# Elementwise work of a four-mixer transformer layer moved from GpSimd to VectorE and ScalarE

## The chip, the cores and the metric

The kernel runs on one core of one Trainium2 chip. The metric is device microseconds of one execution. A core has five engines, each with its own queue of instructions in a fixed order: PE (TensorE, the matmuls; PEld is its weight load), DVE (VectorE), ACT (ScalarE), POOL (GpSimd) and SP (SyncE, which here only issues DMA transfers). An instruction that needs another engine's result waits at the head of its queue, and everything behind it on that engine waits too.

## The reference

One layer over 256 tokens of width 2048, all in f32. Four mixers read slices of `h @ w_in`; their outputs go through a gated merge, an output projection and a feed-forward network with a short convolution.

```python
h = rms_norm(x, attn_norm)
(gla.., lru.., nsa.., rwkv_feat, merge_gate) = split_cols(h @ w_in, IN_SPLITS)
y_a, y_b, y_c, y_d = gla_mixer(..), rglru_mixer(..), nsa_mixer(..), rwkv7_mixer(..)
gates = sigmoid(merge_gate).reshape(B, S, 4, D_MODEL)
merged = zeros_like(x)
for n, y in enumerate((y_a, y_b, y_c, y_d)):
    merged = merged + gates[:, :, n] * (y @ w_branch[n])
x = x + merged @ w_out
u = causal_dwconv(rms_norm(x, ffn_norm) @ ffn_up, ffn_conv_w, ffn_conv_b)
x = x + (silu(u_gate) * u_val) @ ffn_down

# rwkv7_mixer, per head and token, state 64 x 64
k  = k * (1 + (a - 1) * k_a);  kk = normalized(k * k_k)
sa = einsum('ij,j->i', state, -kk_t)
state = state * w_t + outer(sa, kk_t * a_t) + outer(v_t, k_t)
y_t = einsum('ij,j->i', state, r_t)

# gla_mixer, per chunk of 64 tokens
scores = einsum('td,sd,tsd->ts', q, k, exp(b_t - b_s))   # causal
```

## The kernel before

**The stream.** Almost all of the time is weight matmuls. `stream` (L300) loads f32 weights with SP as tiles `raw` of 128x1024 (5 buffers). Each half of a raw is split in two for precision: ACT casts it to `wh` (L327), DVE subtracts to get the rest `wl` (L328), 128x512 each, 6 buffers of either. `group_A` (L337) feeds PE with them: for each 128 rows of the contraction and each 128 output columns a matmul with wh (128x512 moving) and one with wl (128x256), all into a PSUM tile `acc`. One wl, 128x512, holds two blocks of two column pieces, so it serves eight matmuls in a row, four with wh and four with wl. If a wl comes late, PE stands.

**What rides on it.** The mixers' own work lies between these matmuls. In the RWKV7 mixer, `rwkv_kk` (L657) makes kk, k2 and rk, tiles of 128x4x256. `rwkv_blocks` (L714) builds sixteen 64x64 matrices N per half of the partitions, sends them through memory (`n_rows`) to lay 128 blocks of 32x32 on the partitions, and inverts each by a recursion of 31 steps, two operations a step (L742, L743):

```python
self.tt(t, nb[...k + 1:, k], zb[:, k, 0:w], MULT, nc.gpsimd)
self.tt(zb[:, k + 1:, 0:w], zb[:, k + 1:, 0:w], t, ADD, nc.gpsimd)
```

Each reads what the one before wrote. The result goes through memory again (`z_rows`, L746, to Zb), is transposed on DVE in `rwkv_corners` (L758), and feeds 64 small matmuls P on PE. The chain of the state over four chunks (`rwkv_chain`, L818, with the decay sd) follows. In `gla` (L1037) eight levels each compute ge on DVE, its absolute value and exponential on ACT, two products qe (one half on DVE, the other on POOL), 32 small matmuls gs on PE and two masked copies on DVE (L1090). In `nsa` (L1276) the attention's weights pt are scaled by the gates (L1324). `branch` (L1352) adds every branch into merged.

**What sets the order.** The kernel is written in a program order with five bands of priority (load, split, evac, mix, big). A scheduler runs a timeline of its own over it, with its own durations of each instruction, and fixes the order on every engine. Only the transpose of Z (and one other) keeps its place in the program order (L758), between the groups of the first merge. A changed engine or duration therefore moves other instructions too.

Of the kernel before, what the change touches and what calls it, by code (L numbers as in the profile page):

```python
# [14 lines left out]
AF = mybir.ActivationFunctionType  # L15
# [5 lines left out]
P = 128  # L21
# [204 lines left out]
class Kern:  # L226
# [430 lines left out]
    def rwkv_kk(self):  # L657
        nc = self.nc
        hs = self.cst("hs")
        self.hs = hs  # L660
        kk = self.m4("kk")
        for j in range(4):
            nc.gpsimd.tensor_scalar(kk[:, j, :], self.rw_k[:, j, :], self.col("k_k", j), None, op0=MULT)
        sq = self.m4("kksq")
        self.act(sq, kk, AF.Square)

        def pre(out, ps):
            self.ts(out, ps, 1e-24, None, ALU.max)
            self.act(out, out, AF.Sqrt)

        def post(jp, pb):
            self.tt(kk[:, 2 * jp:2 * jp + 2, :], kk[:, 2 * jp:2 * jp + 2, :], pb, MULT)

        self.head_norm(sq, hs, pre, post)
        self.rw_kk = kk

        hka = self.sm([P, 4], "hka")
        self.ts(hka, self.col("k_a", 0, 4), 0.5, None, MULT)
        oka = self.sm([P, 4], "oka")
        self.ts(oka, hka, -1.0, 1.0, MULT, ADD)  # L680
        k2 = self.m4("k2")
        for j in range(4):
            self.act(k2[:, j, :], self.rw_tha[:, j, :], AF.Identity, scale=hka[:, j:j + 1], bias=oka[:, j:j + 1])
        self.tt(k2, k2, self.rw_k, MULT, nc.gpsimd)
        self.rw_k2 = k2
        bb = self.m4("bb")
        self.ts(bb, self.rw_tha, 0.5, 0.5, MULT, ADD)
        self.tt(bb, bb, kk, MULT)
        self.rw_b = bb
        rk = self.m4("rk")  # L690
        self.tt(rk, self.rw_r, k2, MULT, nc.gpsimd)
        self.rw_rk = rk

    def rwkv_ops(self, c):
# [19 lines left out]
    def rwkv_blocks(self, Ts):  # L714


        nc = self.nc
        H = (slice(0, 64), slice(64, 128))
        n = self.m4("N", 16)
        nd = self.pools["d"].tile([16, P, 64], F32, name="n_rows")  # L720
        zd = self.pools["d"].tile([2, 2, 16, 2, 32, 16], F32, name="z_rows")
        for c in range(4):
            ar, bk = Ts[c]["ar"], Ts[c]["bk"]
            pv = self.ps("N")[:, 0:256].rearrange("p (j s) -> p j s", j=4)
            for j in range(4):
                for h in H:
                    self.mm(pv[h, j, :], ar[h, j, 0, :], bk[h, j, 0, :])
            sl = slice(4 * c, 4 * c + 4)
            self.tt(n[:, sl, :], pv, self.cst("mN").unsqueeze(1).broadcast_to([P, 4, 64]), MULT)
            nc.sync.dma_start(nd[sl].rearrange("u p s -> p u s"), n[:, sl, :])  # L730
        nb = self.sb("mg", [P, 32, 32], F32, "N32")
        zb = self.m2("Z32", 32)
        tmp = self.m1("ztmp", 1)[:, 0, :]
        nc.sync.dma_start(self.flat(zb), self.A["z0"])
        for hf in range(2):
            for q in range(2):
                o = 64 * hf + 32 * q
                nc.sync.dma_start(nb[o:o + 32], nd.rearrange("u (a t) s -> (u a) t s", a=2)[:, 32 * q:32 * q + 32, 32 * q:32 * q + 32])
        for k in range(31):
            r, w = 31 - k, min(k + 1, 16)  # L740
            t = tmp[:, 0:r * w].rearrange("p (r w) -> p r w", r=r)
            self.tt(t, nb[:, k + 1:, k:k + 1].broadcast_to([P, r, w]), zb[:, k:k + 1, 0:w].broadcast_to([P, r, w]), MULT, nc.gpsimd)  # L742
            self.tt(zb[:, k + 1:, 0:w], zb[:, k + 1:, 0:w], t, ADD, nc.gpsimd)  # L743
        y = self.m4("Zb", 16)
        nc.gpsimd.memset(y, 0.0)
        nc.sync.dma_start(zd.rearrange("f q u a t s -> (f q u a) t s"), zb)  # L746
        for a in range(2):
            for q in range(2):
                for hf in range(2):
                    o, c0 = 64 * a + 32 * q, 32 * q + 16 * hf  # L750
                    nc.sync.dma_start(y[o:o + 32, :, c0:c0 + 16], zd[hf, q, :, a].rearrange("u t s -> t u s"))
        self.rw_n, self.rw_zb = n, y
# [65 lines left out]
    def rwkv_chain(self, c, T, st):  # L818
# [20 lines left out]
        if c < 3:  # L839
# [8 lines left out]
            else:  # L848
                sd = self.m1("sd")
                ec = self.rw_ec[:, :, c:c + 1]  # L850
                self.tt(sd, st, ec.broadcast_to([P, 4, 64]), MULT, nc.gpsimd)
                self.tt(new, sd, ps, ADD)
        ps = g4("Yo")
        for j in range(4):
# [182 lines left out]
    def gla(self):  # L1037
# [28 lines left out]
        for lv in range(8):  # L1066
# [6 lines left out]
            self.act(e, e, AF.Exp, scale=-1.0 / 16)  # L1073
            qe = self.m4("qe")
            self.tt(qe[:, 0:2, :], qk[:, 0:2, :], e, MULT)
            self.tt(qe[:, 2:4, :], qk[:, 2:4, :], e, MULT, nc.gpsimd)
            if lv == 6:
                for par in range(2):
                    h = H[par]
# [196 lines left out]
    def nsa(self):  # L1276
# [24 lines left out]
        for tt in range(2):  # L1301
# [19 lines left out]
            self.tt(lt, lt, ws[:, :, 0:1].broadcast_to([P, 4, 15]), MULT)  # L1321
            for h in range(4):
                for a in range(2):
                    nc.gpsimd.tensor_scalar(pts[h][:, a, :], pts[h][:, a, :], ws[:, h, 1 + a:2 + a], None, op0=MULT)  # L1324
            srcs = [(None, 0)] + [(a, s) for a in range(2) for s in range(tt + 1)]
            po = self.ps("no")
            for n, (a, st) in enumerate(srcs):
# [24 lines left out]
    def branch(self, n, cg, h, yk, th, first):  # L1352
        ps = self.group_A(self.stream(self.A["w_branch"], (4 * n + cg) * 2 + h, 256, 4), 4, yk)
        with self.at("evac"):
# [6 lines left out]
            else:  # L1361
                b = self.sb("fd", [P, 2, 256], F32, "b")
                self.fold(b, ps)
                self.stt(t, t, 1.0, b, ADD, MULT)
                self.tt(m, m, t, ADD, self.nc.gpsimd)

    def tick(self, most=0):

# [185 lines left out]
```

## Time and profile before

| | |
|---|---|
| median of three runs | 1607.89 us |
| the three runs | 1608.23, 1607.89, 1599.86 us |
| the profiled execution, its own time | 1600.85 us |
| its span in the trace | 1599.1 us |
| PE, DVE, ACT, POOL busy | 98%, 78%, 60%, 11% of the span |
| mean granted TensorE clock | .988 of full speed |

The profiled execution is one of its own, and its span is 1.75 us under its time. In the rows below an operation is read as line, engine, operation, output and inputs by the program's names, shape, and a count. A table by line gives after the bar the busy time in us and the mean of one operation in ns, then the idle time before them and what ended it. A busy time is that in which at least one such operation is under way, so it can be less than count times mean when neighbours overlap. A table of stretches gives the window and its length, then for each engine the busy us and, in brackets, the number of instructions. PEclk is the TensorE clock granted, 1.00 for 2.4 GHz and 0.5 for 1.2 GHz. In a timeline the brackets at the end name the idle time ahead of the instruction and what ended it.

### The profile page before, as it was taken

To read this page: it belongs to the slowest core of one execution; us is meant where nothing else is said; L and a number is where in the kernel's file an instruction comes from. 1 tells how busy PE (TensorE), PEld (TensorE's weight loads), DVE (VectorE), ACT (ScalarE), POOL (GpSimd) and SP (SyncE) were. 2 spreads that over 40 slices of the span, in tenths; PEclk is the share of its full clock that TensorE was granted. 3 is DMA by queue.
4 is the path that set the end of the run, shared out by engine and by line. 5 is a ranking of instruction groups with operands and counts; after the bars stand their busy time and mean duration, and the time that the engine had idled before them with its cause. 6 is when DMAs were issued, how large, how long until landed. Compare 5 with 4: busy or idle time off the path is not lost.

```text
span 1599.1 us, 27514 instructions
## 1 busy us (share of the span) xinstructions
PE 1566.2 (98%) x10062; PEld 1414.7 (88%) x10062; DVE 1248.2 (78%) x2034; ACT 955.8 (60%) x1685; POOL 168.5 (11%) x178
## 2 busy tenths in 40 slices
PE   8999889999899999999999999999999999999998
PEld 7998778888789889899999999999999999999998
DVE  8798965485887768777797888886678886688875
ACT  6777543365665566656566666664466664566653
POOL 3113900000211201311121100000000000000000
PEclk9999988999999999999999999999999999999999
DMA  7656353256356766456676666666666666666663
GB/s 270 233 160 210 121 168 97 96 173 205 124 166 204 239 220 201 156 180 202 202 251 201 194 209 199 201 200 206 198 200 202 201 201 200 202 204 198 200 224 131
DMA packets 95801, 305.80 MB, mean 191 GB/s; under 512 B 20021, under 2 KB 20789, under 8 KB 95664
## 3 DMA queue, kind: packets, MB, share of 16 engines
q1 hardware_dynamic: 94448, 299.60, 58.3%
q0 software_dynamic: 1216, 4.43, 0.8%
q8 instruction: 79, 1.29, 0.3%
q14 instruction: 58, 0.48, 0.1%
HBM read 300.32 MB, written 3.67 MB: 190 GB/s over the span
## 4 chain that ended last, share of the span: by engine, by line
PE 89%; DVE 3%; POOL 3%; issue 2%; DMA 1%; ACT 1%; SPq 1%; DVEq 0%; POOLq 0%; ACTq 0%
PE acc L297 83%; POOL Z L289 2%; POOL ztmp L289 1%; DVE wl L328 1%; PE G L297 1%; PE Yo L297 1%; PE M L297 1%; DMA raw<-in_cmp 0%; PE no L297 0%; DMA raw<-in_wf_r 0%; ACT wh L327 0%; DVE qe L289 0%; PE r L297 0%; PE c L297 0%; PE sc L297 0%
## 5 line engine op out<-in xcount | busy, mean ns | idle before, releaser
L328 DVE TENSOR_TENSOR wl<-raw,wh 128x512 fp32r<-128x512 f32 x1096 | 788.1, 728 | 281.6 <-ACT wh L327 275.8
L297 PE MATMUL acc<-h,wh 128*128 128x512 f32 x3008 | 1000.3, 385 | 1.3 <-DVE th L289 0.9
L327 ACT CAST wh<-raw 128x512 fp32r<-128x512 f32 x1096 | 671.6, 619 | 507.3 <-PE acc L297 474.8
L297 PE MATMUL acc<-h,wl 128*128 128x256 f32 x3008 | 826.9, 275 | 6.1 <-DVE wl L328 6.1
L297 PEld LDWEIGHTS acc<-h,wh 128*128 128x128 f32 x3008 | 571.1, 190 | 83.5 <-issue 1.7
L297 PEld LDWEIGHTS acc<-h,wl 128*128 128x128 f32 x3008 | 579.9, 193 | 10.6 <-DVE wl L328 7.0
L297 PE MATMUL acc<-f,wh 128*128 128x512 f32 x704 | 230.7, 382 | 0.0
L297 PE MATMUL acc<-f,wl 128*128 128x256 f32 x704 | 191.9, 273 | 0.0
L297 PEld LDWEIGHTS acc<-f,wh 128*128 128x128 f32 x704 | 133.1, 189 | 18.5
L297 PEld LDWEIGHTS acc<-f,wl 128*128 128x128 f32 x704 | 135.2, 192 | 0.0
L297 PE MATMUL acc<-mg,wh 128*128 128x512 f32 x256 | 83.9, 382 | 0.3 <-DVE b L289 0.3
L286 DVE SCALAR_TENSOR_TENSOR u<-u,prm,u 128x254 f32<-128x254 f32 (+1 forms) x176 | 80.8, 480 | 0.5
L297 PE MATMUL acc<-mg,wl 128*128 128x256 f32 x256 | 69.6, 273 | 0.0
L289 POOL TENSOR_TENSOR merged<-merged,th 128x512 f32<-128x512 f32 x24 | 41.7, 1736 | 243.7 <-DVE th L286 243.7
L297 PEld LDWEIGHTS acc<-mg,wh 128*128 128x128 f32 x256 | 48.3, 189 | 7.3 <-DVE b L289 0.6
L289 DVE TENSOR_TENSOR xres<-xres,acc 128x512 f32<-128x512 f32 (+1 forms) x66 | 44.0, 668 | 9.9 <-PE acc L297 7.8
L283 ACT ACTIVATE u<-u,prm 128x256 f32<-128x256 f32 x88 | 48.1, 594 | 2.6 <-DVE u L289 0.8
L297 PEld LDWEIGHTS acc<-mg,wl 128*128 128x128 f32 x256 | 49.1, 192 | 0.1
L297 PE MATMUL acc<-wh,h 128*128 128x512 f32 (+1 forms) x128 | 30.2, 328 | 0.0
L289 DVE TENSOR_TENSOR u<-u,rs 128x512 f32<-128x512 f32 x44 | 30.1, 684 | 0.0
L289 DVE TENSOR_TENSOR u<-u,acc 128x512 f32<-128x512 f32 x44 | 30.0, 681 | 0.0
L283 ACT ACTIVATE th<-th 128x512 f32<-128x512 f32 (+1 forms) x33 | 21.3, 645 | 13.5 <-DVE th L289 12.4
(400 smaller groups left out, 1329.3 us busy)
## 6 DMA issues: line engine op xcount, KB each, us to landing
raw<-in_w_up SPq DMA_DIRECT2D x176, 512.0 KB, 4.3
raw<-in_w_gate SPq DMA_DIRECT2D x128, 512.0 KB, 3.6
raw<-in_w_down SPq DMA_DIRECT2D x88, 512.0 KB, 4.2
raw<-in_w_branch SPq DMA_DIRECT2D x32, 512.0 KB, 3.9
raw<-in_w_out SPq DMA_DIRECT2D x32, 512.0 KB, 4.2
raw<-in_wf_k SPq DMA_DIRECT2D x8, 512.0 KB, 4.4
raw<-in_wf_misc SPq DMA_DIRECT2D x8, 512.0 KB, 4.4
raw<-in_wf_lx SPq DMA_DIRECT2D x8, 512.0 KB, 4.3
```

The source lines that it names most:

```text
L283: return self.nc.scalar.activation(out, in_, func, bias=bias, scale=scale, **kw)
L286: return self.nc.vector.scalar_tensor_tensor(out, in0, scalar, in1, op0=op0, op1=op1)
L289: return (eng or self.nc.vector).tensor_tensor(out, a, b, op=op)
L297: return self.nc.tensor.matmul(out, lhsT, rhs, start=start, stop=stop, **kw)
L327: nc.scalar.copy(wh, rb)
L328: nc.vector.tensor_tensor(wl, rb, wh.bitcast(F32), op=SUB)
```

## The change

Seven pieces of elementwise work change their engine. From POOL to DVE go the product of k2 with k and rk (two of 128x1024), the recursion's 62 operations, the state decay sd (two small ones), the second half of every qe (eight of 128x512) and the addition into merged (24 of 128x512). From POOL to ACT go the four scalings of kk (128x256) and the sixteen scalings of pt (128x128 and 128x256). What is computed stays the same.

```diff
--- before.py
+++ after.py
@@ -660,7 +660,7 @@
         self.hs = hs
         kk = self.m4("kk")
         for j in range(4):
-            nc.gpsimd.tensor_scalar(kk[:, j, :], self.rw_k[:, j, :], self.col("k_k", j), None, op0=MULT)
+            self.act(kk[:, j, :], self.rw_k[:, j, :], AF.Copy, scale=self.col("k_k", j))
         sq = self.m4("kksq")
         self.act(sq, kk, AF.Square)
 
@@ -681,14 +681,14 @@
         k2 = self.m4("k2")
         for j in range(4):
             self.act(k2[:, j, :], self.rw_tha[:, j, :], AF.Identity, scale=hka[:, j:j + 1], bias=oka[:, j:j + 1])
-        self.tt(k2, k2, self.rw_k, MULT, nc.gpsimd)
+        self.tt(k2, k2, self.rw_k, MULT)
         self.rw_k2 = k2
         bb = self.m4("bb")
         self.ts(bb, self.rw_tha, 0.5, 0.5, MULT, ADD)
         self.tt(bb, bb, kk, MULT)
         self.rw_b = bb
         rk = self.m4("rk")
-        self.tt(rk, self.rw_r, k2, MULT, nc.gpsimd)
+        self.tt(rk, self.rw_r, k2, MULT)
         self.rw_rk = rk
 
     def rwkv_ops(self, c):
@@ -739,8 +739,8 @@
         for k in range(31):
             r, w = 31 - k, min(k + 1, 16)
             t = tmp[:, 0:r * w].rearrange("p (r w) -> p r w", r=r)
-            self.tt(t, nb[:, k + 1:, k:k + 1].broadcast_to([P, r, w]), zb[:, k:k + 1, 0:w].broadcast_to([P, r, w]), MULT, nc.gpsimd)
-            self.tt(zb[:, k + 1:, 0:w], zb[:, k + 1:, 0:w], t, ADD, nc.gpsimd)
+            self.tt(t, nb[:, k + 1:, k:k + 1].broadcast_to([P, r, w]), zb[:, k:k + 1, 0:w].broadcast_to([P, r, w]), MULT)
+            self.tt(zb[:, k + 1:, 0:w], zb[:, k + 1:, 0:w], t, ADD)
         y = self.m4("Zb", 16)
         nc.gpsimd.memset(y, 0.0)
         nc.sync.dma_start(zd.rearrange("f q u a t s -> (f q u a) t s"), zb)
@@ -848,7 +848,7 @@
             else:
                 sd = self.m1("sd")
                 ec = self.rw_ec[:, :, c:c + 1]
-                self.tt(sd, st, ec.broadcast_to([P, 4, 64]), MULT, nc.gpsimd)
+                self.tt(sd, st, ec.broadcast_to([P, 4, 64]), MULT)
                 self.tt(new, sd, ps, ADD)
         ps = g4("Yo")
         for j in range(4):
@@ -1073,7 +1073,7 @@
             self.act(e, e, AF.Exp, scale=-1.0 / 16)
             qe = self.m4("qe")
             self.tt(qe[:, 0:2, :], qk[:, 0:2, :], e, MULT)
-            self.tt(qe[:, 2:4, :], qk[:, 2:4, :], e, MULT, nc.gpsimd)
+            self.tt(qe[:, 2:4, :], qk[:, 2:4, :], e, MULT)
             if lv == 6:
                 for par in range(2):
                     h = H[par]
@@ -1321,7 +1321,7 @@
             self.tt(lt, lt, ws[:, :, 0:1].broadcast_to([P, 4, 15]), MULT)
             for h in range(4):
                 for a in range(2):
-                    nc.gpsimd.tensor_scalar(pts[h][:, a, :], pts[h][:, a, :], ws[:, h, 1 + a:2 + a], None, op0=MULT)
+                    self.act(pts[h][:, a, :], pts[h][:, a, :], AF.Copy, scale=ws[:, h, 1 + a:2 + a])
             srcs = [(None, 0)] + [(a, s) for a in range(2) for s in range(tt + 1)]
             po = self.ps("no")
             for n, (a, st) in enumerate(srcs):
@@ -1362,7 +1362,7 @@
                 b = self.sb("fd", [P, 2, 256], F32, "b")
                 self.fold(b, ps)
                 self.stt(t, t, 1.0, b, ADD, MULT)
-                self.tt(m, m, t, ADD, self.nc.gpsimd)
+                self.tt(m, m, t, ADD)
 
     def tick(self, most=0):
```

POOL's queue goes from 165 rows to 65, DVE's from 1912 to 2001, ACT's from 1582 to 1588. The scheduler also moves what lies around. On DVE, where the recursion begins (N_166 is N laid out anew, Z_167 the result being built up, rw_v the values of the mixer), the difference of after against before:

```order
 L328 TENSOR_TENSOR wl_1937<-raw_1922,wh_1936 128x512
-L286 SCALAR_TENSOR_TENSOR rw_v_1951<-F_1734,prm,rw_v_1951 128x255
+L286 SCALAR_TENSOR_TENSOR rw_v_1951<-F_1734,prm,rw_v_1951 128x255 x2
+L289 TENSOR_TENSOR ztmp_1115<-N_166_1113,Z_167_1114 128x31
+L289 TENSOR_TENSOR Z_167_1114<-Z_167_1114,ztmp_1115 128x31
+L289 TENSOR_TENSOR ztmp_1115<-N_166_1113,Z_167_1114 128x60
+L289 TENSOR_TENSOR Z_167_1114<-Z_167_1114,ztmp_1115 128x30x2
+L289 TENSOR_TENSOR ztmp_1115<-N_166_1113,Z_167_1114 128x87
+L289 TENSOR_TENSOR Z_167_1114<-Z_167_1114,ztmp_1115 128x29x3
 L328 TENSOR_TENSOR wl_1965<-raw_1962,wh_1964 128x512
+L289 TENSOR_TENSOR ztmp_1115<-N_166_1113,Z_167_1114 128x112
+L289 TENSOR_TENSOR Z_167_1114<-Z_167_1114,ztmp_1115 128x28x4
```

The first step, which waits for N's way through memory, now stands in DVE's queue ahead of wl_1965 and of everything behind it. From there on one to three steps stand between two wl, the last just behind wl_2689.

On DVE at the transpose of Z (merged_321 and th_1960 belong to the first merge), before:

```order
L328 TENSOR_TENSOR wl_2461<-raw_2446,wh_2460 128x512
L289 TENSOR_TENSOR merged_321_2316<-merged_321_2316,acc_2289 128x512
L286 SCALAR_TENSOR_TENSOR merged_321_2316<-th_1960,merged_321_2316 128x512
L758 STREAM_TRANSPOSE Z_2320<-Zb_1183 128x1024
L328 TENSOR_TENSOR wl_2475<-raw_2472,wh_2474 128x512
```

and after:

```order
L328 TENSOR_TENSOR wl_2755<-raw_2752,wh_2754 128x512
L328 TENSOR_TENSOR wl_2767<-raw_2752,wh_2766 128x512
L328 TENSOR_TENSOR wl_2786<-raw_2783,wh_2785 128x512
L758 STREAM_TRANSPOSE Z_2320<-Zb_1183 128x1024
L328 TENSOR_TENSOR wl_2798<-raw_2783,wh_2797 128x512
```

The transpose has moved behind 22 more wl. On PE the matmuls P move with it: they stood 251 rows behind the start of acc_1961, the accumulation that wl_1965 feeds first, and stand 427 behind it now, all of the added rows being weight matmuls. The last matmuls of N stand 18 PE rows later than before. On SP the transfer z_rows now stands behind thirteen more weight loads.

On DVE in the GLA loop, one level (gqk holds q and k, gst the scores), before:

```order
L289 TENSOR_TENSOR ge_5378<-gb_4223 128x512
L1090 COPY_PREDICATED gst_5297<-gm,gs_5331 128x256
L1090 COPY_PREDICATED gst_5298<-gm,gs_5332 128x256
L328 TENSOR_TENSOR wl_4430<-raw_4415,wh_4429 128x512
L328 TENSOR_TENSOR wl_4450<-raw_4447,wh_4449 128x512
L289 TENSOR_TENSOR qe_5382<-gqk_3534,ge_5378 128x512
```

and after:

```order
L289 TENSOR_TENSOR ge_5378<-gb_4223 128x512
L328 TENSOR_TENSOR wl_4450<-raw_4447,wh_4449 128x512
L328 TENSOR_TENSOR wl_4462<-raw_4447,wh_4461 128x512
L289 TENSOR_TENSOR qe_5382<-gqk_3534,ge_5378 128x512 x2
L328 TENSOR_TENSOR wl_4476<-raw_4473,wh_4475 128x512
L1090 COPY_PREDICATED gst_5297<-gm,gs_5358 128x256
L1090 COPY_PREDICATED gst_5298<-gm,gs_5359 128x256
```

Both products of a level stand on DVE in a row, a level holds three wl, and its copies have moved behind its products. On PE there were 11 to 22 weight matmuls between two groups gs, and there are 20 to 25 now.

## Rows read from the trace of the kernel before

**Rows 1.** Page: busy time of PE, and the chain that ended last by line.

```profile
PE 1566.2 (98%) x10062; PEld 1414.7 (88%) x10062; DVE 1248.2 (78%) x2034; ACT 955.8 (60%) x1685; POOL 168.5 (11%) x178
...
PE acc L297 83%; POOL Z L289 2%; POOL ztmp L289 1%; DVE wl L328 1%; PE G L297 1%; PE Yo L297 1%; PE M L297 1%; DMA raw<-in_cmp 0%; PE no L297 0%; DMA raw<-in_wf_r 0%; ACT wh L327 0%; DVE qe L289 0%; PE r L297 0%; PE c L297 0%; PE sc L297 0%
```

**Rows 2.** Stretches: us, busy PE PEld DVE ACT POOL, PEclk, DMA share, GB/s.

```profile
170.00:180.00 10.00, 5.14 (x19) 4.27 (x18) 10.00 (x10) 0.67 (x2) 9.21 (x11) 0.73 0.34 101
180.00:190.00 10.00, 10.00 (x57) 8.97 (x57) 10.00 (x13) 7.75 (x13) 9.22 (x11) 0.93 0.47 150
...
210.00:220.00 10.00, 7.62 (x85) 6.84 (x86) 8.63 (x17) 3.40 (x6) 0.00 (x0) 0.55 0.71 261
...
420.00:430.00 10.00, 6.87 (x97) 5.86 (x96) 9.40 (x15) 4.69 (x9) 2.54 (x2) 1.00 0.33 107
...
840.00:880.00 40.00, 40.00 (x246) 36.77 (x245) 31.05 (x47) 23.76 (x41) 5.73 (x5) 1.00 0.62 204
```

**Rows 3.** PE's timeline: start, length, operation, in brackets the idle time before.

```profile
155.98 0.27 PE L297 MATMUL acc<-h,wl 128*128 128x256 f32 x1
...
167.82 0.38 PE L297 MATMUL acc<-h,wl 128*128 128x256 f32 x1 [1.20 <-DVE wl L328]
...
175.57 0.58 PE L297 MATMUL acc<-h,wl 128*128 128x256 f32 x1 [4.86 <-DVE wl L328]
...
212.38 1.92 PE L297 MATMUL P<-Z,N 32*32 32x32 f32 x64 [5.65 <-DVE Z L758]
...
423.62 0.69 PE L297 MATMUL gs<-qe 64*64 64x64 f32 x32 [0.91 <-DVE qe L289]
...
428.47 0.69 PE L297 MATMUL gs<-qe 64*64 64x64 f32 x32 [2.22 <-DVE qe L289]
```

**Rows 4.** DVE by line and shape: wl from 60 to 100, then 150 to 202.

```profile
L328 DVE TENSOR_TENSOR wl<-raw,wh 128x512 fp32r<-128x512 f32 x29 | 19.4, 695 | 3.5 <-ACT wh L327 3.5
...
L328 DVE TENSOR_TENSOR wl<-raw,wh 128x512 fp32r<-128x512 f32 x32 | 28.6, 930 | 3.7 <-ACT wh L327 3.7
```

**Rows 5.** Stretch: POOL's operations with tile Z alone, busy us and count.

```profile
147.00:202.00 55.00, 48.49 (x62) 0.94 0.42 135
```

**Rows 6.** Timelines of DVE and, where its name stands, POOL.

```profile
103.73 5.85 DVE L328 TENSOR_TENSOR wl<-raw,wh 128x512 fp32r<-128x512 f32 x3 [2.14 <-ACT wh L327]
...
421.65 1.27 POOL L289 TENSOR_TENSOR qe<-gqk,ge 128x512 f32<-128x512 f32 x1 [4.14 <-ACT ge L283]
...
421.68 1.79 DVE L289 TENSOR_TENSOR qe<-gqk,ge 128x512 f32<-128x512 f32 x1
```

**Rows 7.** DVE by line and shape: prices of single operations, mean in ns.

```profile
L289 DVE TENSOR_TENSOR hidt<-hidt,hid 128x15 f32<-128x15 f32 x2 | 0.3, 171 | 0.0
...
L289 DVE TENSOR_TENSOR ops<-bb,eneg 128x256 f32<-128x256 f32 x4 | 1.6, 408 | 0.0
...
L289 DVE TENSOR_TENSOR ge<-gb 128x512 f32<-128x512 f32 x8 | 5.4, 678 | 0.0
...
L289 DVE TENSOR_TENSOR yc<-yc,rw_g 128x1024 f32<-128x1024 f32 x1 | 1.2, 1218 | 0.0
```

**Rows 8.** PE's waits over the span: total us, times, longest.

```profile
PE gs L297 <- DVE qe L289: 7.0, 5, 2.2
```

**Rows 9.** DVE's timeline: two independent operations in a row.

```profile
127.51 0.41 DVE L289 TENSOR_TENSOR ops<-rw_r,ein 128x256 f32<-128x256 f32 x1
127.84 0.41 DVE L289 TENSOR_TENSOR ops<-bb,eneg 128x256 f32<-128x256 f32 x1
```

**Rows 10.** Timelines of POOL, SP and DVE: the recursion's two ends.

```profile
148.00 0.45 POOL L289 TENSOR_TENSOR ztmp<-N,Z 128x31 f32<-128x31 f32 x1 [16.09 <-DMA N<-n_rows]
...
201.30 0.33 SPq L746 DMA_DIRECT2D z_rows<-Z  x1
...
211.08 1.25 DVE L758 STREAM_TRANSPOSE Z<-Zb 128x1024 f32<-128x1024 f32 x1 [8.56 <-DMA Zb<-z_rows]
```

**Rows 11.** ACT by line and shape: exponentials over the pt tiles.

```profile
L283 ACT ACTIVATE pt<-pt,nm 128x256 f32<-128x256 f32 x8 | 4.0, 502 | 0.0
```

## The prediction

> **What bounds the kernel now.** I read the page first, then a table of stretches, then the timelines of the engines in the stretches where TensorE stands. On the page the reader is to see that TensorE (PE) is busy 98% of the span and that its weight matmuls own 83% of the chain that ended last, while GpSimd (POOL), 11% busy, still owns 3% of that chain with the inverse recursion (tiles Z and ztmp) [rows 1]. So moving POOL's work can pay only where PE stands. The table of stretches says where that is not: from 840 to 880 us PE is busy 40.00 of 40 with 246 matmuls, which is 0.1626 us a matmul at full clock [rows 2]. The merge, whose 24 additions are moved, runs largely in such stretches. What can be won lies in two places.
>
> The first is the recursion, 148 to 222 us. DVE is busy 10.00 of 10 there while PE has 5.14 of 10 [rows 2]. PE waits three times: 1.20 and 4.86 us for a wl (VectorE's half of the weight split), 5.65 us for Z, 11.7 us in all [rows 3]. And the granted clock falls to its lower level behind each long wait. From 170 to 180 the mean is .73, so 5.4 us were at half; PE worked at half from 175.57 on, 4.4 us, and another 1.4 us after 180 (.93), so 5.8 us of work lost 2.9. From 210 to 220 the mean .55 means 9.0 us at half, 6.6 of them worked from 212.38 on: 3.3 lost. Together the place loses 11.7 + 6.2 = **17.9 us**.
>
> The reason for the wl waits is to be seen in two tables: a wl takes 669 ns of DVE time each from 60 to 100 us (19.4 / 29) and 894 from 150 to 202 us (28.6 / 32) [rows 4], beneath 62 POOL steps that fill 48.49 of 55 us [rows 5]. The sharpest row is a pair in the GLA stage: a DVE qe that starts 0.03 us after a POOL qe of 1.27 takes 1.79 [rows 6], where the same shape takes 0.68 elsewhere [rows 7]. So the two engines hold each other up when both read two SBUF operands.
>
> The second place is the GLA loop, 410 to 460 us. From 420 to 430, about two levels of it, PE is busy 6.87 of 10 and DVE 9.40; PE waits 7.0 us in five waits for qe [rows 2, 8].
>
> **The change part by part.** *Recursion on DVE.* It takes 62 dependent steps of 16 to 256 elements a partition, 9552 elements together. DVE's prices are 0.171 us at 15 elements and 0.408 at 256 [rows 7], a line of 0.156 + 0.000983 N: 62 x 0.156 + 9552 x 0.000983 = **19.1 us**. The ends: independent 128x256 operations start 0.33 apart though each lasts 0.41 [rows 9], so 19.1 less 62 x 0.075 is 14.5 at best; and 62 x 0.41 = 25.3 if every step costs as the largest does. I take 19.1, since each step reads what the one before wrote and waits for it. The Trainium skill, "VectorE: DVE Perf Modes", section "The DRAIN you can't avoid", says that the next DVE operation does not start until the pipe of the one before is empty. By that rule 19.1 would hold even without the dependence; the rows [rows 9] show independent operations overlapping, so here only the dependence speaks for it, and by the rows without it the sum would be 14.5.
>
> Where do the 19.1 us lie? In the new order they stand among 48 wl and 24 other operations. POOL no longer disturbs these: 48 wl at .669 = 32.1; twelve 128x512 additions and four other operations of that size at .68 = 10.9; five of 128x1024 at 1.22 = 6.1; four scans and one operation of about 128x256 at .41 = 2.0. With the recursion that is 51.1 + 19.1 = 70.2 us. PE needs 8 matmuls for a wl, so for those 48 it needs 62.4. Start: POOL began at 148.00 when N had come back from memory [rows 10]; in the new order the last N matmul stands 18 PE rows later, so 148.0 + 18 x 0.1626 = 150.9. Six steps (1.3) and one wl stand ahead of the wl that PE wants at 155.98 [rows 3], ready at 152.9: 3.1 us of cover. The last wl is then ready at 150.9 + 70.2 - 0.2 = 220.9, wanted at 155.98 + 47 x 1.30 = 217.1: **PE stands 3.8 us** for wl in pieces. Behind the last step SP carries Z to memory and back: 201.30 to 211.08, 9.8 us, and PE's P starts 1.3 after that [rows 3, 10]. So Z is there at 221.1 + 11.1 = 232.2. P was 251 PE rows behind the start of that acc before and is 427 now, so PE arrives at 155.8 (the row ahead of 155.98) + 427 x 0.1626 + 3.8 = 229.0 and **waits 3.2**. SP's z_rows transfer moves with it, behind thirteen more weight loads, which were queued behind its wait for Z before and are not any more; the weight loads had five buffers of room there, so 0. With a shorter wait I charge half of the second clock loss again, 1.6. Gain: 17.9 - 3.8 - 3.2 - 1.6 = **9.3**. Bounds: at 14.5 no wl is late and P waits 2.4, gain 13.9, and 17.9 if even that wait is hidden; at 25.3 the gain is gone (second rival).
>
> *qe on DVE.* Before, 4.85 us lie between the starts of two gs groups; PE works half of 6.87, 3.4, of them and DVE half of 9.40, 4.7, of which a qe held to 1.79 [rows 2, 3, 6]. After, the order puts two qe of .68 and one wl more into a level: 4.7 + 1.36 - 1.79 + .67 = 4.9. Between two gs groups PE now has 20 to 25 acc matmuls where it had 11 to 22, some 24 x 0.1626 + 0.7 for gs = 4.6 of a level of about 5.0, since PE's gs also waits through ACT's two steps on ge. Idle time per level falls from 1.4 to about 0.4, five levels: **5.0**. Bounds 0 (ACT's steps and two qe in a row set the level) and 7.0 (all of the wait goes).
>
> *k2 and rk on DVE*: two of 1.22, so 2.4 us more; against it, three wl beneath those POOL operations took 5.85 us where three at .669 take 2.0 [rows 6]. Between +2.4 and -3.8 of DVE time, PE not waiting there: 0. *merged*: 24 x .68 = 16.3 us more DVE work where PE stands nowhere and DVE has 31.05 of 40 [rows 2]: 0; without that slack it would be up to 16. *kk and pt on ACT*: at most 20 x .502 = 10 us [rows 11] on an engine busy 60%: 0, up to +2 if a wh cast behind sixteen pt scalings comes late. *sd*: two small operations, 0.
>
> **Sum.** 9.3 + 5.0 = 14.3 off the profiled execution's 1600.85 (span 1599.1) is 1586.6; off the median 1607.89 it is 1593.6. The three runs lie at two places, two near 1608 and one near 1600 as the profile; weighing 2 to 1, the base is 1605.5 and the forecast **1591**.
>
> **The rivals.** *GLA stays as it is.* Both qe on one engine are in series before gs, and ACT's two steps in front are unchanged. Then only the 9.3: 1596.2. For it speaks DVE's 9.40 of 10; against it that the held qe loses 1.1 us a level and that the order gives PE more to do between.
>
> *DVE becomes the bound in the recursion.* If a step costs .41 whatever its size, DVE needs 76.4 us where PE needs 62.4. PE then stands 10.0 for wl, 3.2 for Z, and the whole clock loss of 6.2 returns: 17.9 - 19.4 = -1.5, with GLA's 5.0 a gain of 3.5: 1602.0. For it: DVE is already at 10.00 of 10 there. Against it: the row of 171 ns for 15 elements.
>
> *The chain of steps is as slow on DVE as on POOL*, each step held by its wait for the step before. A step at p costs PE 3.8 + 62p - 19.1 for wl; with 3.2 and 6.2 as above the total gain is 13.5 less that, which is a loss over 8.0 us from p = .59 on. At POOL's mean of 48.49 / 62 = .78 [rows 5] it is 1625. Against it: POOL's steps are long partly because DVE holds them up, and no DVE row of such size comes near .59.
>
> That the change doesn't do what it says is ruled out: POOL's order shrinks from 165 rows to 65, and the steps stand on DVE.
>
> **How the numbers follow.** Chances: forecast .60, GLA as it is .19, DVE the bound .15, slow chain .06. 0.5% is 8.0 us, about what a measurement of this kernel can tell from no change: faster means below 1599.9, slower above 1615.9. Faster: .60 + .19 = .79; same .15; slower .06. The range: at its best the forecast gives 17.9 + 7.0 = 24.9 off the lower of the two places, 1576; upward it takes in GLA as it is (off the median 1598.6) and ends at the centre of DVE the bound, 1602. What is left out above, about half of .15 and .06, and a little below, is under 2 in 10.
>
> **What would show it.** Right: in the recursion a wl falls from 894 ns toward 670, the steps on DVE sum to 14 to 25 us, PE's waits for wl and Z there add to about 7 us instead of 11.7, and the granted clock keeps above .9 near 175; in GLA PE is busy over 8.5 of 10 with waits for qe under 3 us; from 690 us on PE is as full as before. Wrong: ztmp steps over .41, a wait of PE for wl longer than 5 us, PE waits behind the merge's additions, or a half-clock stretch at a place that had none.

## The result, and the profile after

The changed kernel takes 1583.79 us (median of 4 runs, 1580.59 to 1585.06) beside 1608.06 us for the kernel before (4 runs, 1599.86 to 1610.69). The ratio is 0.9856, with a 95% interval of 0.9836 to 0.9876. The profiled execution took 1582.63 us with a span of 1580.8; against the profiled execution of before, 1600.85 and 1599.1, that is 18.3 us less span. 14.3 were forecast on that base. In a later job the changed kernel came out at 1576.75 us, ratio 0.9815 (0.9782 to 0.9849), so its own gain, 24 and 30 us on the medians, is known to within some 5 us.

The page of the changed kernel, busy times and the chain that ended last by line, which answers to [rows 1]:

```profile
PE 1562.0 (99%) x10062; PEld 1413.0 (89%) x10062; DVE 1238.8 (78%) x2132; ACT 962.7 (61%) x1705; POOL 38.7 (2%) x60
...
PE acc L297 89%; PE G L297 1%; PE Yo L297 1%; DVE wl L328 1%; DVE qe L289 0%; PE M L297 0%; PE no L297 0%; DMA raw<-in_wf_r 0%; PE r L297 0%; PE c L297 0%; ACT wh L327 0%; DVE th L289 0%; PE sc L297 0%; ACT ge L283 0%; PE ptp L1332 0%
```

DVE took on a hundred instructions and is busy for 9 us less than before. POOL has left the chain. PE idles for 1580.8 - 1562.0 = 18.8 us where it idled for 1599.1 - 1566.2 = 32.9: 14.1 of the 18.3 us are waits that are gone, and the other 4.2 are work that ran at a higher clock. PE's waits over the span, changed kernel (total us, times, longest), which answer to [rows 3, 8]:

```profile
PE acc L297 <- DVE th L289: 3.0, 2, 1.6
PE gs L297 <- DVE qe L289: 2.5, 5, 0.8
PE gy L297 <- DVE qe L289: 1.4, 1, 1.4
...
PE P L297 <- DVE Z L758: 0.7, 1, 0.7
```

The wait of acc for wl, 6.1 us before, is no longer in the list. That for Z has shrunk from 5.65 to 0.7, that of gs for qe in the GLA loop from 7.0 to 2.5. Two have grown: acc for th, from 0.9 to 3.0 us, in which a new accumulation waits until DVE has emptied the PSUM tile that it is to use, and that of gy, the matmuls of the seventh of the eight levels, for its qe, from 0.5 (then POOL's) to 1.4. The lines of before:

```profile
PE acc L297 <- DVE th L289: 0.9, 1, 0.9
...
PE gy L297 <- POOL qe L289: 0.5, 1, 0.5
```

The two places by stretches of the changed kernel (columns as in [rows 2]):

```profile
160.00:170.00 10.00, 10.00 (x63) 9.21 (x62) 10.00 (x19) 8.02 (x13) 0.00 (x0) 1.00 0.67 206
170.00:180.00 10.00, 10.00 (x64) 9.21 (x63) 10.00 (x19) 7.79 (x13) 0.00 (x0) 1.00 0.49 159
180.00:190.00 10.00, 8.67 (x54) 7.71 (x52) 9.93 (x21) 5.77 (x11) 0.00 (x0) 1.00 0.84 259
...
220.00:230.00 10.00, 9.27 (x113) 8.33 (x113) 5.46 (x9) 4.42 (x8) 0.00 (x0) 1.00 0.71 154
...
410.00:420.00 10.00, 9.31 (x111) 7.86 (x109) 9.79 (x19) 6.68 (x12) 0.00 (x0) 1.00 0.48 154
420.00:430.00 10.00, 6.74 (x73) 5.80 (x73) 9.10 (x19) 6.90 (x16) 0.54 (x1) 0.86 0.51 161
430.00:440.00 10.00, 10.00 (x55) 8.73 (x55) 6.97 (x11) 4.33 (x9) 0.00 (x0) 0.80 0.45 146
```

In the recursion DVE is as full as before, 10.00 of 10, but it does 19 instructions in 10 us from 160 to 180 where it did 10 or 11, and PE is served: 10.00 with 64 matmuls at full clock from 170 to 180, where it had 5.14 with 19 at .73. In the GLA loop PE gains from 410 to 420, but from 420 to 430 it is busy 6.74 of 10, no more than the 6.87 of before, and a half-clock stretch (the granted clock at its lower level) that was not there before stands from 420 to 440 (.86, .80). It begins at 427.1 us, behind the first of the two waits that have grown and within the second:

```profile
425.49 0.93 PE L297 MATMUL gy<-qe 64*64 64x64 f32 x16 [1.41 <-DVE qe L289]
...
427.86 0.80 PE L297 MATMUL acc<-h,wh 128*128 128x512 f32 x1 [1.44 <-DVE th L289]
```

The recursion itself: DVE's wl by line and shape from 150 to 202 us, answering to [rows 4], and the stretch with DVE's operations on ztmp alone (the 62 steps; busy us, count):

```profile
L328 DVE TENSOR_TENSOR wl<-raw,wh 128x512 fp32r<-128x512 f32 x40 | 26.9, 681 | 0.1
...
140.00:240.00 100.00, 19.43 (x62) 1.00 0.66 194
```

The steps took 19.43 us where 19.1 were worked out, and a wl takes 26.9 / 40 = 0.67 us of DVE time again instead of 0.89. The ends of the recursion on DVE, SP and PE in the changed kernel, answering to [rows 3, 10], with a stretch of DVE's order in between:

```profile
148.31 0.21 DVE L289 TENSOR_TENSOR ztmp<-N,Z 128x31 f32<-128x31 f32 x1 [0.87 <-DMA N<-n_rows]
...
149.38 0.25 DVE L289 TENSOR_TENSOR ztmp<-N,Z 128x87 f32<-128x87 f32 x1
149.67 0.25 DVE L289 TENSOR_TENSOR Z<-Z,ztmp 128x87 f32<-128x87 f32 x1
149.84 0.69 DVE L328 TENSOR_TENSOR wl<-raw,wh 128x512 fp32r<-128x512 f32 x1
150.44 0.27 DVE L289 TENSOR_TENSOR ztmp<-N,Z 128x112 f32<-128x112 f32 x1
...
190.25 0.48 PE L297 MATMUL acc<-h,wh 128*128 128x512 f32 x1 [1.58 <-DVE th L289]
...
212.67 0.17 DVE L289 TENSOR_TENSOR Z<-Z,ztmp 128x16 f32<-128x16 f32 x1
...
213.16 0.42 SPq L746 DMA_DIRECT2D z_rows<-Z  x1
...
225.86 1.25 DVE L758 STREAM_TRANSPOSE Z<-Zb 128x1024 f32<-128x1024 f32 x1 [3.90 <-DMA Zb<-z_rows]
...
227.16 1.20 PE L297 MATMUL P<-Z,N 32*32 32x32 f32 x64 [0.73 <-DVE Z L758]
```

### The profile page after: what moved, and what is told of

It is laid out like the page before. It is cut to its first block, busy times and chain, and to the rows that moved or that the text cites. A ratio compares the mean times of both kernels' runs of the same rounds, so it can differ in the third digit from the quotient of the medians.

```text
span 1580.8 us, 27481 instructions
## 1 busy us (share of the span) xinstructions
PE 1562.0 (99%) x10062; PEld 1413.0 (89%) x10062; DVE 1238.8 (78%) x2132; ACT 962.7 (61%) x1705; POOL 38.7 (2%) x60
## 4 chain that ended last, share of the span: by engine, by line
PE 95%; DVE 2%; ACT 1%; issue 1%; DMA 1%; SPq 0%; DVEq 0%; ACTq 0%
PE acc L297 89%; PE G L297 1%; PE Yo L297 1%; DVE wl L328 1%; DVE qe L289 0%; PE M L297 0%; PE no L297 0%; DMA raw<-in_wf_r 0%; PE r L297 0%; PE c L297 0%; ACT wh L327 0%; DVE th L289 0%; PE sc L297 0%; ACT ge L283 0%; PE ptp L1332 0%
## 5 line engine op out<-in xcount | busy, mean ns | idle before, releaser
L328 DVE TENSOR_TENSOR wl<-raw,wh 128x512 fp32r<-128x512 f32 x1096 | 757.7, 698 | 278.7 <-ACT wh L327 272.1
L380 ACT COPY u<-acc 128x512 f32<-128x512 f32 x44 | 25.5, 579 | 0.0
L297 PEld LDWEIGHTS acc<-wh,h 128*128 128x128 f32 x128 | 23.2, 202 | 2.1 <-issue 0.4
```

The costliest lines, as they stand in the source:

```text
L297: return self.nc.tensor.matmul(out, lhsT, rhs, start=start, stop=stop, **kw)
L328: nc.vector.tensor_tensor(wl, rb, wh.bitcast(F32), op=SUB)
L380: self.nc.scalar.copy(dst, ps[0:rows, :, 0])
```

## The experiments

Two numbers are used for each kernel beside its time, since the runs of one kernel scatter by some 15 us. The span times its mean granted clock, here *full-clock time*, is what the span would be if everything took twice as long at the lower of the clock's two levels, at half clock; the rest of the span is the *clock's share*. This is a measure and not exact: a wait, and by the last section a small matmul, does not take twice as long there, and the clock is known to .001, which is 1.6 us of span. Over 31 runs of the kernel before in one job the full-clock time scatters by 3 us and the clock's share by 18 (9.6 to 27.3); over the 7 and 19 runs of the two other jobs the full-clock time scatters by 5 and 7. So most of the scatter is the clock's, and a saved wait is read best from the first number. The medians:

| kernel | us | ratio to before, 95% | full-clock time | clock's share |
|---|---|---|---|---|
| before, three jobs | 1605.2, 1606.5, 1604.2 | 1 | 1582.5, 1582.2, 1582.7 | 20.8, 22.5, 19.2 |
| changed | 1583.8 | .9856 (.9836 to .9876) | 1566.4 | 15.0 |
| changed, again | 1576.8 | .9815 (.9782 to .9849) | 1565.3 | 9.4 |
| before + recursion moved | 1592.4 | .9924 (.9899 to .9949) | 1572.2 | 19.1 |
| before + qe moved | 1603.5 | 1.0000 (.9978 to 1.0023) | 1576.8 | 24.8 |
| before + merged moved | 1605.1 | 1.0009 (.9983 to 1.0035) | 1581.6 | 21.6 |
| before + the rest moved | 1606.3 | 1.0027 (1.0001 to 1.0052) | 1580.9 | 24.9 |
| changed, recursion back | 1601.0 | .9973 (.9948 to .9998) | 1575.0 | 24.8 |
| changed, qe back | 1584.3 | .9856 (.9820 to .9892) | 1571.7 | 10.3 |
| changed, merged back | 1579.9 | .9832 (.9795 to .9869) | 1567.9 | 10.3 |
| changed, the rest back | 1588.0 | .9907 (.9872 to .9942) | 1567.7 | 19.0 |
| changed, sd back | 1580.5 | .9865 (.9822 to .9907) | 1565.4 | 14.2 |
| changed + idle two-operand POOL work | 1599.9 | .9968 (.9944 to .9992) | 1582.1 | 16.8 |
| changed + idle one-operand POOL work | 1585.9 | .9871 (.9838 to .9903) | 1569.9 | 14.3 |

**Recursion alone, moved.**

```diff
-  self.tt(t, nb[..], zb[..], MULT, nc.gpsimd)
-  self.tt(zb[..], zb[..], t, ADD, nc.gpsimd)
+  self.tt(t, nb[..], zb[..], MULT)
+  self.tt(zb[..], zb[..], t, ADD)
```

> The kernel before with the recursion alone moved to VectorE (its 62 steps), all else as before. Theory A, from the two traces: the recursion carries nearly all of the gain, since PE's idle time from 120 to 240 us fell from 12.4 to 2.6 us and the half-clock time there, worth 6.2 us, is gone: 14 to 17 us less than before. Theory B, the terms of the prediction: 9.3 us less, the rest being GLA's. Both: the 62 steps take about 19.4 us of VectorE and no wait of PE for a wl is over 2 us in that place.

It gained 12.8 us on the medians, between the two theories' numbers (the interval, 8 to 16 us, has room for either); 10.3 of it are full-clock time and 1.7 the clock's. The steps took 19.50 us and the longest wait for wl was 1.0. So the recursion carries 10 of the 16 us of waits, and the waits did go as theory A says; the clock's share hardly came down with them.

**Recursion back on POOL in the changed kernel.** The same edit, the other way.

> The changed kernel with the recursion alone back on GpSimd. Theory A: nearly all of the gain is gone, 14 to 17 us over the changed kernel, with waits of PE for wl of 4 us or more and a half-clock stretch near 175 us. Theory B, the prediction's terms: 9.3 us over the changed kernel.

It lost 17 us against 1583.8 (1.2% of the ratio, some 19 us, when each is set against its own runs of before): 8.6 to 9.7 of full-clock time and the rest the clock's. PE's waits in it:

```profile
PE acc L297 <- DVE wl L328: 7.0, 4, 3.5
PE P L297 <- DVE Z L758: 6.2, 1, 6.2
```

Both waits of before are back, though everything else is on the new engines. Theory A's size is right; of its details a single wait of 4 us did not come, it is four of up to 3.5.

**What hurts: POOL's long chain, or POOL's presence?** To the changed kernel 62 POOL operations of the recursion's shapes are added that work on tiles nobody reads. The order of the four other engines stays that of the changed kernel, row by row.

```diff
+  nc.gpsimd.memset(dz, 0.0)
   ...
+  for k in range(31):
+      q = nb if k == 0 else dz
+      self.tt(t, q[:, k + 1:, 0:1]..., dz[:, k:k + 1, 0:w]..., MULT, nc.gpsimd)
+      self.tt(dz[:, k + 1:, 0:w], dz[:, k + 1:, 0:w], t, ADD, nc.gpsimd)
```

> The changed kernel with 62 operations of the recursion's shapes added on GpSimd, on scratch tiles that nobody reads, starting when N has landed; the order on the other engines is that of the changed kernel. Theory A, contention: the mere presence of GpSimd operations with two operands in SBUF stretches VectorE's work there. The wl mean from 150 to 200 us goes back from about 0.67 toward 0.9 us, the recursion on VectorE takes over 25 us, PE waits 5 to 15 us for wl or Z, and the time is 6 to 20 us over the changed kernel. Theory B, the serial chain: the kernel before lost its time because GpSimd's chain of steps was long, not because it disturbed VectorE. Then wl stays below 0.72 us, and the time is that of the changed kernel within 2 us.

16 us slower: work that nobody needs, on an otherwise empty engine, takes back 15.7 us of full-clock time. PE's waits; then DVE by line and shape from 150 to 200 us for wl, from 150 to 195 for an operation with one operand alone and one with an operand in PSUM; then the 62 steps on DVE:

```profile
PE acc L297 <- DVE wl L328: 11.9, 10, 3.2
PE acc L297 <- DVE th L289: 3.9, 2, 2.5
...
L328 DVE TENSOR_TENSOR wl<-raw,wh 128x512 fp32r<-128x512 f32 x25 | 22.3, 906 | 0.0
...
L293 DVE TENSOR_SCALAR th<-th 128x1024 f32<-128x1024 f32 x1 | 1.1, 1110 | 0.0
...
L289 DVE TENSOR_TENSOR th<-th,acc 128x512 f32<-128x512 f32 x1 | 0.7, 675 | 0.0
...
140.00:240.00 100.00, 24.90 (x62) 1.00 0.58 166
```

A wl is at 0.9 us again, the steps at 24.9, and PE waits 11.9 us for wl. Theory B, the serial chain, falls as the reason for the late wl: no result waits for these operations. Theory A holds, but for one bound: the steps stretched to 24.9, not over 25. The wait of P for Z did not come back, though; it is 5.65 us before and 6.2 with the recursion back on POOL. So that part is not shown to be contention: it goes with the end of POOL's own chain, and how long this chain would be there undisturbed was not tried. The last rows say whom POOL's work hits. The DVE operation with th and acc reads one operand from PSUM and takes 675 ns beneath it, as it does without it (674 to 681 ns in the other kernels), while those with two operands in SBUF are stretched. But so is th from th, an operation with a single operand, in SBUF: 1110 ns here and 1083 in the kernel before, 684 in the changed kernel.

**The same with one operand on POOL's side.** Again 62 operations of these shapes on idle tiles, each a product with a constant.

```diff
-      self.tt(t, q[..], dz[..], MULT, nc.gpsimd)
-      self.tt(dz[..], dz[..], t, ADD, nc.gpsimd)
+      self.ts(t, q[..], 0.0, None, MULT, eng=nc.gpsimd)
+      self.ts(dz[..], t, 0.0, None, MULT, eng=nc.gpsimd)
```

> The changed kernel with 62 GpSimd operations of the recursion's shapes on scratch tiles, as in the run before with such operations, but each reads one operand only (a product with a constant). The order on the other engines is that of the changed kernel. Theory A, any GpSimd operation that reads SBUF holds up VectorE operations with two SBUF operands: wl from 150 to 200 us again near 0.9 us until the 62 are done, PE waits for wl, time 5 to 16 us over the changed kernel. Theory B, both sides must read two operands: wl near 0.68, time as the changed kernel within 2 us.

It lies between the theories: 3.5 to 4.6 us of full-clock time more; on the median 9 us beside the changed kernel of the same job, which is within theory A's, but only 2 beside that of the first, the clock's share included. POOL's busy time from 140 to 240 us (with tile dt), and DVE's wl from 150 to 200 us:

```profile
140.00:240.00 100.00, 51.60 (x62) 0.97 0.62 179
...
L328 DVE TENSOR_TENSOR wl<-raw,wh 128x512 fp32r<-128x512 f32 x32 | 23.5, 746 | 1.1 <-ACT wh L327 1.1
```

POOL was busy for 51.6 us, longer than the 45.2 us of the two-operand work, yet a wl rose only to 746 ns (681 without, 906 with two operands). PE waits 2.1 us for wl and 5.3 for th. A POOL operation with one operand, here a product with a constant, does hold up DVE: for a wl at less than a third of the price, for the 62 steps at about half (22.0 us where the two-operand work made it 24.9, and 19.4 without).

**qe alone, moved; and qe back in the changed kernel.**

```diff
-  self.tt(qe[:, 2:4, :], qk[:, 2:4, :], e, MULT, nc.gpsimd)
+  self.tt(qe[:, 2:4, :], qk[:, 2:4, :], e, MULT)
```

> The kernel before with the second half of every qe alone moved to VectorE. Theory A: PE's wait for qe falls from 7.0 to about 2.5 us, as in the changed kernel, but a half-clock stretch follows in the same place and takes most of it back: 0 to 2 us less than before. Theory B, the prediction's term: 5.0 us less, no half-clock stretch from 410 to 460 us.

> The changed kernel with the second half of every qe back on GpSimd. Theory A, as the run with qe moved alone showed (waits 5.7 us less, half-clock time 4 us more): the waits of PE for qe are back near 7 us, the half-clock stretch at 425 to 437 us is gone, and the time is 0 to 3 us over the changed kernel. Theory B, the prediction's term: 5.0 us over it.

Moved alone it changed the time by nothing that can be told (1.0000): full-clock time fell by 5.7 us and the clock's share rose by 4.0. The stretches 400 to 440 and 440 to 480 us of that run:

```profile
400.00:440.00 40.00, 39.39 (x374) 34.81 (x372) 32.58 (x56) 27.79 (x48) 0.31 (x1) 1.00 0.50 155
440.00:480.00 40.00, 36.37 (x282) 31.75 (x282) 30.72 (x49) 26.98 (x49) 3.58 (x4) 0.91 0.45 141
```

The waits are less, and the lower clock (.91 of 40 us is 7.2 us at half) stands behind them, as theory A says. Here too it begins, at 451.8, with the waits of gy and of acc for th, 1.40 and 1.44 us, which end at 450.3 and 452.7. Back on POOL it cost 7.6 us on the median: 6.4 of full-clock time, with the wait for qe at 7.0 us as before and no half-clock stretch from 400 to 480 us (the waits of gy and acc there are 0.45 and 0.88 us), and 0.9 of the clock's share. There theory B is nearer, though beside the changed kernel of the first job the median is only 0.6 us more. So the waits that qe's move takes away are worth 5.7 to 6.4 us in either surrounding; how much of that the clock takes back differs.

**merged alone, moved; and merged back.**

```diff
-  self.tt(m, m, t, ADD, self.nc.gpsimd)
+  self.tt(m, m, t, ADD)
```

> The kernel before with the 24 additions into merged alone moved to VectorE. Theory A: wl beside them get shorter but PE never waits there: within 2 us of the kernel before. Theory B, contention costs everywhere: 3 us or more less than before, in line with the 3 us by which the changed kernel with merged back on GpSimd was slower.

> The changed kernel with the 24 additions into merged back on GpSimd. Theory A: VectorE's wl near them get longer, but PE does not wait for them, since VectorE has slack there: within 2 us of the changed kernel. Theory B: the contention costs wherever GpSimd reads two operands beside VectorE: 24 x 1 us of VectorE time lost, of which some 5 us or more reach PE.

Alone it did nothing (1.0009, 0.9983 to 1.0035). Back on POOL it was 3.2 us slower on the median of the same job, 2.6 of them full-clock time, with no wait of PE over 1 us that the changed kernel does not have. The intervals overlap, and beside the first job's changed kernel it is 3.9 us faster, so a gain of some 3 us from this piece stays open; of theory B's 5 us or more full-clock time shows nothing, its farthest runs of the two kernels lying 4.5 us apart. The contention itself is there, as both theories have it: DVE's wl from 690 to 1000 us with merged back on POOL, and in the changed kernel:

```profile
L328 DVE TENSOR_TENSOR wl<-raw,wh 128x512 fp32r<-128x512 f32 x237 | 176.1, 754 | 49.4 <-ACT wh L327 47.7
...
L328 DVE TENSOR_TENSOR wl<-raw,wh 128x512 fp32r<-128x512 f32 x237 | 167.8, 715 | 51.8 <-ACT wh L327 50.6
```

DVE idles some 50 us before these wl in either, so the 8 us are taken from its slack.

**kk, k2, rk, sd and pt: alone, back, and sd alone back.**

```diff
-  nc.gpsimd.tensor_scalar(kk.., col("k_k", j), None, op0=MULT)
+  self.act(kk.., AF.Copy, scale=col("k_k", j))
-  self.tt(k2, k2, self.rw_k, MULT, nc.gpsimd)      # rk and sd likewise
+  self.tt(k2, k2, self.rw_k, MULT)
-  nc.gpsimd.tensor_scalar(pts.., ws.., None, op0=MULT)
+  self.act(pts.., AF.Copy, scale=ws..)
```

> The kernel before with kk, k2, rk, sd and the scalings of pt alone moved. Theory A: the waits for wl and Z in the recursion stay (about 12 us), so the time is the kernel before's within 3 us. Theory B: half-clock time in the state chain falls and 5 to 12 us are gained.

> The changed kernel with kk, k2, rk, sd and the scalings of pt back on GpSimd; recursion, qe and merged stay on VectorE. Theory A (the waits decide, and these pieces stand where PE does not wait): PE's waits as in the changed kernel, time within 3 us of it. Theory B: these pieces are what lowered the loss at the lower clock in the state chain from 240 to 320 us (before 17, changed kernel 10 to 14 us of half-clock time in the profiles; with the recursion alone moved 38): then the half-clock time there is 25 us or more and the time 5 to 12 us over the changed kernel.

> The changed kernel with the state decay sd alone back on GpSimd (two operations of 0.62 us instead of 0.42). Theory A: sd is off the chain that PE waits for, within 2 us of the changed kernel. Theory B: it stands in the state chain, whose half-clock stretches grow by it: 3 us or more over it.

Alone: 2 us slower on the medians, 1.0027 (1.0001 to 1.0052), with the waits for wl and Z as before; that is theory A. Back: 1.3 to 2.4 us of full-clock time, and a clock's share of 19.0 instead of 9.4 to 15.0. The state chain, 280 to 320 us, in the changed kernel and with the rest back:

```profile
280.00:320.00 40.00, 40.00 (x301) 32.48 (x301) 17.38 (x35) 11.11 (x23) 1.17 (x3) 0.91 0.27 84
...
280.00:320.00 40.00, 40.00 (x228) 31.61 (x227) 11.24 (x22) 7.50 (x15) 0.06 (x1) 0.66 0.16 53
```

From .91 to .66, that is from 7 to 27 us at half clock: this is theory B's sign, and the time, 4 and 11 us over the changed kernel of the two jobs, is near its 5 to 12. But sd alone back left all as in the changed kernel (1565.4 of full-clock time, 14.2 of the clock's), so it isn't the length of sd. What goes with the clock in all thirteen kernels of the table is PE's order in the chain. Seven of them (before, each of the four pieces moved alone, recursion back, the rest back) have one order: at one place the small matmuls S and Yo that end a round are followed at once by the next round's M and G. The other six (the changed kernel, qe, merged or sd back, and the two with idle POOL work) have another: four of M's matmuls stand earlier, among S and Yo, and six weight matmuls stand between M and G. The clock's share is 19.0 to 24.9 us in the first order and 9.4 to 16.8 in the second. That place in the trace of before and in that of the changed kernel, PE's timelines:

```profile
266.17 0.34 PE L297 MATMUL S<-uv,tk 128*64 128x64 f32 x4
...
268.69 0.33 PE L297 MATMUL Yo<-mt,uv 128*64 128x64 f32 x2
...
271.04 3.09 PE L297 MATMUL M<-ops 64*128 64x128 f32 x16
274.06 0.47 PE L297 MATMUL G<-uv,mt 128*64 128x64 f32 x2
...
280.51 0.58 PE L297 MATMUL acc<-yb,wl 128*128 128x256 f32 x1
```

```profile
284.66 1.17 PE L297 MATMUL M<-ops 64*128 64x128 f32 x12
285.76 0.48 PE L297 MATMUL acc<-h,wh 128*128 128x512 f32 x1
...
286.74 0.27 PE L297 MATMUL acc<-h,wl 128*128 128x256 f32 x1
286.94 0.33 PE L297 MATMUL G<-uv,mt 128*64 128x64 f32 x2
```

Before, nothing but small matmuls runs from 266.2 to 280.5 us, and the granted clock is .51 from 270 to 280. In the changed kernel it is 1.00 from 280 to 290, and it falls there too, at 290.6 among the matmuls G, but for 3.4 us instead of 13.7. That the order is the cause was not tried by itself; the scheduler changed it along with the rest, so it stays a correlation over thirteen kernels.

**The changed kernel again.**

> The changed kernel itself once more, beside the runs of this job, for more runs of it: 1580 to 1587 us. Theory A: its gain over the kernel before is about 16 us of time that PE stood (waits), and the rest, up to 6 us, is a smaller loss at the lower clock, which scatters from run to run.

1576.75 us, below what was expected; full-clock time 1565.3, within 1.1 of the first time, and a clock's share of 9.4 instead of 15.0. Against its own runs of before, 16.9 us are waits and 13.1 the clock. None of the kernels tried is clearly faster than the changed kernel.

## Why the prediction was right, step by step

**The place and the mechanism.** The gain was forecast where PE stands, in the recursion and the GLA loop, and from POOL's disturbance of DVE. The added idle work showed the mechanism for the late wl, and the runs with one piece moved alone showed the places: 10.3 and 5.7 us of full-clock time, beside 16.1 to 16.9 for the whole change. The two other pieces read 1.1 and 1.8 alone, so the four do not simply add up.

**Recursion, forecast 9.3.** In the traces PE's idle time from 120 to 240 us fell by 9.8 us (12.4 to 2.6), and the 6.2 of the clock there went altogether, so that for this place the term should have been near 16. Moved alone the recursion gave 12.8, since much of the clock's share came back in the state chain (38 us at half clock there in its profile, 17 in that of before). Its parts:
- The steps: 19.1 forecast, 19.43 measured as busy time. The line through two prices held. What each takes of DVE is the distance to the next start, and there the dependence shows: in the rows above a step starts 0.04 us after the end of the one that it reads, while a wl starts 0.08 before the end of the step ahead of it. The distances of the 62 come to 17.7 us, since two out of three steps have other work behind them.
- The other operations among them: 51.1 forecast. From the first step to the end of the last it is 212.84 - 148.31 = 64.5 us where 70.2 were worked out, and 46.8 of it are the distances of these. This term was mis-sized: they were priced by how long an operation lasts (0.68), and a wl and what follows it start 0.60 apart. The row that shows it [rows 9] was used for a bound on the steps and not for these.
- The start: 150.9 forecast, 148.31 measured. The eighteen rows by which N's matmuls moved cost nothing: N's last operation on DVE began at 135.8, and at 136.3 before, where PE's wait of 0.7 us for N's operands, now gone, lay ahead of it.
- So no wl was late, where 3.8 us were forecast. Instead PE waited 1.58 us for th, which DVE emptied late. This wait was not in the sum, which counted only wl as what DVE owes PE.
- Z: its way through memory took 12.7 us (213.16 to 225.86) instead of 9.8, but it left 8 us earlier than worked out; P waited 0.7 instead of 3.2. The half of a clock loss that was charged did not come.

**qe, forecast 5.0.** Waits worth 5.7 and 6.4 us went in the two runs; in the two traces PE's idle time from 360 to 480 went from 9.0 to 5.5 us. The size of the waits was about right. That a half-clock stretch comes with it, 6.8 us from 427.1 on, was not in the sum; at up to 3.4 us it takes back what the trace shows as gained there. It is a sign that was listed as wrong, and of the signs listed as right one failed: PE over 8.5 of 10 does not hold from 420 to 430.

**The others, forecast 0.** merged is 0 in time alone and some 3 at most in company. k2, rk, kk, sd and pt are worth about 2 us of full-clock time. Moved together with the recursion they also bring the order that goes with a smaller clock's share; no term had that.

**The rivals.** *GLA as it is* is true of the time of qe moved alone and not of its waits. *DVE becomes the bound*: the steps averaged 0.31 us, not .41; DVE is full at 10.00 of 10 but delivers. *The slow chain* needed .59. Errors of the sum went both ways, and that it came out near is in part luck: between the two profiles the recursion's place gave about 6 us more than its term, GLA's 5.0 was nearly used up by the clock there, and what remains of the 18.3 is the clock in the state chain (17 us at half clock before, 10 to 14 after), which no term had.

**Overlap of steps, and contention.** The Trainium skill, "VectorE: DVE Perf Modes", section "The DRAIN you can't avoid", was weighed for the steps. It also says that a next operation that is not held starts earlier, which the prediction left out. The trace fits both, though it does not show what holds a step: a step starts 0.04 us behind the end of the step that it reads, and operations that do not depend on each other start 0.60 apart while lasting 0.69. The Trainium skill, "SBUF — State Buffer", section "Who interferes with whom", states that a DVE instruction with two SBUF inputs contends with a GpSimd instruction that reads SBUF, that the port pair they share is an exclusive lock, and that a DVE instruction with at most one SBUF input does not contend outside the 2-port perf modes. The 675 ns of the operation with a PSUM operand agree with the last; whether the stretched th with its single operand ran in such a mode, no run here shows. For the lock the runs differ: POOL's one-operand work, which also reads SBUF and lasted longer, held a wl at less than a third of the price of the two-operand work.

## What to carry to other kernels

Elementwise work on GpSimd, above all with two SBUF operands, is not free while VectorE is the engine that TensorE waits for: look for VectorE operations whose mean grows beneath it, and count what VectorE loses before counting what it would have to take over. Here it took over 62 steps of 19.4 us and still got ahead. Price what an engine does in a row by the distance of starts, not by the length of an operation (and dependent operations apart from independent ones), and let the sum hold every thing that the engine owes the bound one, evacuations too. Where runs of a kernel scatter, split the span into full-clock time and clock's share before judging a change of under 1%.

## What the runs showed of the hardware that was not expected

- Most of the scatter of this kernel's runs is TensorE's clock: over 31 runs of before in one job the clock's share went from 9.6 to 27.3 us while the full-clock time kept within 1581.3 to 1584.4; over 19 in another it was 11.1 to 29.0 and 1580.2 to 1586.9.
- The lower clock costs small matmuls less than weight matmuls: pairs of G follow each other by 0.40 us at the lower level (from 274.06 us in the kernel before) and by 0.26 at full (from 286.94 in the changed kernel), a factor of 1.5; a wh and wl of the weights by 0.64 and 0.33, nearly 2.
- A GpSimd operation that reads one SBUF operand disturbs VectorE far less than one that reads two (wl at 746 and 906 ns, 681 without), though it kept GpSimd busy longer (51.6 and 45.2 us).
- A VectorE operation with a single operand, in SBUF, can be stretched by GpSimd too: th from th, 128x1024, took 684 ns without GpSimd's work, 837 beneath the one-operand and 1110 beneath the two-operand work. One with an operand in PSUM kept its 675.
